# Output projections: a third of the weight tiles' low halves subtracted on GpSimd, and sums of squares added source by source

## The chip, the cores and the metric
The kernel runs on one core of a Trainium2 chip. The metric is the device time of one execution in microseconds (us), lower is better. Three timed runs of the kernel before gave 2628.65, 2626.24 and 2626.40 us, so the median is 2626.4 us. The execution that the profiler recorded took 2624.79 us, of which the span from the first to the last recorded instruction is 2623.0 us.

## The reference
The program computes two layers of a trunk over 256 latent tokens of width 2048, all in f32. Layer 0 is attention, layer 1 a long convolution ("hyena"); each ends in an output projection, and each is followed by a gated feed-forward block (ffn). What matters here:

```
xs = xs + g1 * (mix @ w_out)                       # output projection, 2048 x 2048; layer 0: attn_w_out, layer 1: hy_w_out
h  = rms(xs, norm2_g) * (1 + sc2) + sh2            # needs mean(xs^2) per token, over all 2048 columns
xs = xs + g2 * ((gelu(dwconv(h @ w_gate)) * (h @ w_val)) @ w_down)
```

g1, sc2, sh2 and g2 are vectors made by the "ada" products, s_lat @ ada_w + ada_b, one per layer and kind.

## The kernel before, in words
Every activation stands transposed, columns on the 128 partitions and 256 tokens along the free axis, as 16 pieces of 128x256. Each f32 product is made as three products of rounded halves: x = xh + xl and w = wh + wl, and wh*xh + wh*xl + wl*xh is summed in PSUM.

**One weight tile** is 256 rows by 512 columns of a weight matrix, stored as 128x1024 f32 (512 KB). `wload` (L326) issues its DMA from SyncE's queue into one of 6 `raw` buffers. `wsplit` (L331) makes the two halves: ScalarE rounds raw to `whi` (L334), VectorE subtracts, `wlo` = raw - whi (L335). There are three `whi` and three `wlo` buffers. `products` (L338) then issues 24 matmuls on TensorE for one tile, 8 with wh and xh, 8 with wh and xl, and 8 with wl and xh last, so `wlo` is wanted 16 matmuls after `whi`.

**The two output projections** are calls of `proj_out` (L1017), at L1163 with `w_out` and at L1321 with `hw_out`. Each has 32 weight tiles: a first pass over three groups of 512 rows, for one half of the columns and then the other (24 tiles), and a second pass over the last group (8 tiles). In the last group of a pass two tiles are taken together, and each column piece is finished by `evac` (L1023): VectorE multiplies the PSUM result by the gate and adds it to `xs` (L1026). In the second pass the piece is squared as well, on ScalarE; the first twelve squares are added up on VectorE into one tile, `sqacc` (L400), the last four stay single (L1030).

**What runs beside them.** `drive` (L315) calls generators between weight tiles. In both projections these are the ada products on VectorE (L486, a multiply with accumulation over 128x1024 f32, both inputs in SBUF), at 0.8 and 0.6 per step. Beside the first projection runs the end of attention (softmax and transposes) and, in its second pass, the filters of the convolution ("fill", L581 to L619: products on TensorE, multiplications and splits on VectorE and ScalarE). Beside the second runs the last of the convolutions ("conv", L1223).

**The sums of squares.** `rstd_of` (L376) sums over the partitions by matmuls: five sources (`sqacc` and four squares), each in two halves of 128 tokens, with the 128x128 piece as the weights and one column of ones as the moving operand. It goes through all sources for tokens 0 to 127, then again for tokens 128 to 255. VectorE reads the two columns (L384) and finds the reciprocal root in ten small steps (`newton`, L361); two matmuls (L391) spread it over the partitions, and `Normed.get` (L409) makes the input of the next stage. Nothing of the next stage's products can start before that.

**Order of the work.** The order on each engine is laid down when the program is built, by a list scheduler with priorities and a cost for each operation; `tc.high_priority()` and `tc.issue_after` (L485) steer it. At run time each engine works in that order and waits on semaphores. GpSimd has no work in the kernel after its first microsecond.

Of the kernel before, what the change touches and what calls it, by code (L numbers as in the profile page):

```python
# [16 lines left out]
ALU = mybir.AluOpType  # L17
AX = mybir.AxisListType

P = 128  # L20
# [175 lines left out]
def trunk_kernel(ctx, tc, out, xT, cT, cols, rows, f_w0, f_w12, f_w3, ada_w, ada_t, w_in, w_out, hw_in, hw_out,  # L196
                 wg, wv, wd, k_tab, k_fg, k_z, k_decay):
    nc = tc.nc
    V, A, PE, SP, G = nc.vector, nc.scalar, nc.tensor, nc.sync, nc.gpsimd
# [7 lines left out]
    def nm(s):  # L207
        uid[0] += 1
        return f"{s}{uid[0]}"
# [4 lines left out]
    def s2(shape, dt=F32, name="s"):  # L214
        return pool.tile(shape, dt, tag="s2", bufs=NS2, name=nm(name))
# [7 lines left out]
    def tiny(shape, name="t"):  # L223
        return pool.tile(shape, F32, tag="tiny", bufs=40, name=nm(name))
# [24 lines left out]
    def keep(shape, name, dt=F32):  # L249
        return pool.tile(shape, dt, tag=name, name=nm(name))  # L250
# [6 lines left out]
    ones = keep([P, P], "ones")  # L257
# [50 lines left out]
    def need(*what):  # L308
        for lj in what:
            ada_bg.drain(lj)  # L310
# [4 lines left out]
    def drive(gen, rate, ada_rate=0.0):  # L315
        up = isinstance(ada_rate, tuple)
        for now in gen:
            if now == "down":
                up = False
                continue  # L320
            ada_bg.step(0.0 if calm[0] else ada_rate if not isinstance(ada_rate, tuple) else ada_rate[0] if up else ada_rate[1])
            ev_bg.step(EV_RATE)
            fill_bg.step(fill_rate[0])
            bg.step(rate)

    def wload(src, tag="raw"):  # L326
        raw = pool.tile([P, 2, 512], F32, tag=tag, bufs={"raw": NRAW, "araw": NAR}.get(tag, NW), name=nm(f"raw_{lab[0]}_"))
        SP.dma_start(raw, src)
        return raw

    def wsplit(raw):  # L331
        hi = pool.tile([P, 2, 512], F32R, tag="whi", bufs=NW, name=nm(f"whi_{lab[0]}_"))
        lo = pool.tile([P, 2, 512], F32R, tag="wlo", bufs=NW, name=nm(f"wlo_{lab[0]}_"))
        A.copy(hi, raw)  # L334
        V.tensor_tensor(lo, raw, hi, op=ALU.subtract)  # L335
        return hi, lo

    def products(terms):  # L338
# [12 lines left out]
    def turn(bank):  # L351

        for i in range(4):
            with tc.issue_after(last(PE)):
                PE.transpose(bank[:, i * P:(i + 1) * P], ident, ident)
# [5 lines left out]
    def newton(y, v, n):  # L361

        t = small(n)
        V.tensor_scalar(t.bitcast(I32), v.bitcast(I32), 1, None, op0=ALU.logical_shift_right)
        V.tensor_scalar(y.bitcast(I32), t.bitcast(I32), -1, 0x5F1FFFF9, op0=ALU.mult, op1=ALU.add)

        V.tensor_tensor(t, y, y, op=ALU.mult)
        V.scalar_tensor_tensor(out=t, in0=t, scalar=-0.703952253, in1=v, op0=ALU.mult, op1=ALU.mult)
        V.scalar_tensor_tensor(out=y, in0=t, scalar=0.703952253 * 2.38924456, in1=y, op0=ALU.add, op1=ALU.mult)
        V.tensor_tensor(t, y, y, op=ALU.mult)  # L370
        V.tensor_tensor(t, t, v, op=ALU.mult)
        V.scalar_tensor_tensor(out=t, in0=t, scalar=-10.0 / 3.0, in1=t, op0=ALU.add, op1=ALU.mult)
        V.tensor_scalar(t, t, 0.375, 1.875, op0=ALU.mult, op1=ALU.add)
        V.tensor_tensor(y, y, t, op=ALU.mult)

    def rstd_of(accs, ps):  # L376

        pss = ps()
        n = len(accs)
        for tt in range(2):  # L380
            for i, a in enumerate(accs):
                PE.matmul(pss[:, tt: tt + 1], a[:, tt * P:(tt + 1) * P], ones[:, 0:1], start=i == 0, stop=i == n - 1)
        v = tiny([P, 2])
        V.tensor_scalar(v, pss[:, 0:2], 1.0 / D, EPS, op0=ALU.mult, op1=ALU.add)  # L384
        y = tiny([P, 2])
        newton(y, v, 2)
        pb = ps()
        dg = s2([P, T])
        for tt in range(2):
            V.tensor_scalar(dg[:, tt * P:(tt + 1) * P], ident, y[:, tt: tt + 1], None, op0=ALU.mult)  # L390
            PE.matmul(pb[:, tt * P:(tt + 1) * P], ones, dg[:, tt * P:(tt + 1) * P], start=True, stop=True)  # L391
        return pb[:, 0:T]

    def square_into(acc, x, first):
        if first:
            A.activation(acc, x, AF.Square)
        else:
            sq = s2([P, T])
            A.activation(sq, x, AF.Square)
            V.tensor_tensor(acc, acc, sq, op=ALU.add)  # L400
# [616 lines left out]
    def proj_out(w, passes, xsplit, gate, xs, accs, hook=lambda half, left: None):  # L1017


        acc = pool.tile([P, T], F32, tag="sqacc", bufs=2, name=nm("sqacc"))  # L1020
        accs.append(acc)

        def evac(final, half, banks, ct):  # L1023
            g = half * 8 + ct
            xt = xs[g // 4][:, g % 4]
            V.scalar_tensor_tensor(out=xt, in0=banks[ct // 2][:, (ct % 2) * T:(ct % 2 + 1) * T], scalar=gate[:, g:g + 1], in1=xt, op0=ALU.mult, op1=ALU.add)  # L1026
            if final and g < 12:
                square_into(acc, xt, g == 0)
            elif final:
                accs.append(s2([P, T], F32, "sq"))  # L1030
                A.activation(accs[-1], xt, AF.Square)

        def term(banks, ct, wh, wl, k2, xh, xl, k, first, last):
            c = ct % 4
            return (banks[ct // 2][:, (ct % 2) * T:(ct % 2 + 1) * T], wh[:, k2, c * P:(c + 1) * P], wl[:, k2, c * P:(c + 1) * P],
                    xh[:, k], xl[:, k], first, last)

        for p, (order, rings) in enumerate(passes):
            final = p == len(passes) - 1
            n = len(order)  # L1040
            for half in range(2):
                lab[0] = f"proj{p}{half}"
                banks = rings[half].four()
                if n > 3:
                    turn(banks[0])
                for i, kg in enumerate(order):
                    calm[0] = final and half == 1 and i == n - 1
                    if final:
                        hook(half, n - 1 - i)
                    xh, xl = xsplit(kg)  # L1050
                    src = lambda sub, j: w[kg * 2 + sub, half * 2 + j]
                    if i < n - 1:
                        for sub in range(2):
                            for j in range(2):
                                wh, wl = wsplit(wload(src(sub, j)))
                                products(term(banks, j * 4 + c, wh, wl, k2, xh, xl, sub * 2 + k2,
                                              i == 0 and sub * 2 + k2 == 0 and c % 2 == 0, False)
                                         for k2 in range(2) for c in range(4))
                                yield
                    else:  # L1060
                        for j in range(2):
                            ws = [wsplit(wload(src(sub, j))) for sub in range(2)]
                            for c in range(4):
                                ct = j * 4 + c
                                products([term(banks, ct, *ws[k // 2], k % 2, xh, xl, k, n == 1 and k == 0 and ct % 2 == 0, k == 3)
                                          for k in range(4)])
                                if c % 2:
                                    with tc.high_priority() if final else nullcontext():
                                        evac(final, half, banks, ct - 1)
                                        evac(final, half, banks, ct)  # L1070
                                    yield
# [50 lines left out]
    accs = []  # L1122
# [16 lines left out]
    def fill(dcs, at, rate):  # L1139

        def hook(*now):
            ftag[0] = HI4 if now[0] == 0 else LO4
            if dcs and now == at:
                fill_bg.add(filters(dcs), "fill")
                fill_bg.one()
                fill_rate[0] = rate
        return hook
# [12 lines left out]
        fill_rate[0] = 0.0  # L1160

    need((0, 2))
    drive(proj_out(w_out, OUT_PASSES, o_split, adaV[:, 0, 2], xs, accs, fill(DCS[1], (0, 0), FILL1)), O_RATE, O_ADA)  # L1163
    need((0, 2), (0, 3), (0, 4))
    g2 = gain_of(col("n2", 0, KT), adaV[:, 0, 4], "g2")
    main_done()
# [7 lines left out]
    accs = []  # L1174
# [143 lines left out]
        xs.append(t)  # L1318
    accs = []
    need((1, 2))  # L1320
    drive(proj_out(hw_out, OUT_PASSES, h2split, adaV[:, 1, 2], xs, accs), HO_RATE, HO_ADA)  # L1321
    need((1, 3), (1, 4))
    g2 = gain_of(col("n2", KT, KT), adaV[:, 1, 4], "g2b")
    with tc.high_priority():
# [24 lines left out]
```

## Time and profile before

| | |
|---|---|
| median of 3 runs | 2626.4 us |
| the profiled execution | 2624.79 us |
| its span | 2623.0 us |
| TensorE busy in the span | 2523.8 us (96%) |
| VectorE busy | 1965.9 us (75%) |
| ScalarE busy | 1258.7 us (48%) |
| GpSimd busy | 0.7 us |
| first output projection, about | 520 to 692 us |
| second output projection, about | 1758 to 1888 us |

In the rows the engines are PE (TensorE's matmuls), PEld (its weight loads), DVE (VectorE), ACT (ScalarE), POOL (GpSimd) and SP (SyncE). L335 is line 335 of the kernel. A group such as "wlo_proj<-raw_proj,whi_proj" says which tile is written and which are read; "idle before" is the time in which the engine stood still just before the instruction, with the engine and tile that ended it. Matmuls are pipelined: a matmul row starts when the one before it has gone in, so that the distance of two starts is the cost of one, and the duration in the row is longer.

### The profile page before, as it was taken

What the parts mean: (1) busy time and instruction counts of PE and PEld (TensorE: products, weight loads), DVE (VectorE), ACT (ScalarE), POOL (GpSimd) and SP (SyncE); (2) the same over time, 40 slices, a digit from 0 to 9 for tenths busy, and PEclk for the clock granted to TensorE, in tenths of its full rate; (3) what the DMA queues carried; (4) which work ended last, traced back from release to release, by engine and by line L of the source; (5) the groups of instructions that cost most, each with busy time, mean ns of one, the idle gap of its engine ahead of it and who ended that gap; (6) DMA issues with size and microseconds to landing.
All of it is one profiled execution on the core that took longest, in us unless ns stands there. A gap on an engine that the chain in (4) does not pass through costs nothing. (4 is left out here: it accounts for less than half of the span.)

```text
span 2623.0 us, 48116 instructions
## 1 busy us (share of the span) xinstructions
PE 2523.8 (96%) x19502; PEld 2349.2 (90%) x19502; DVE 1965.9 (75%) x3071; ACT 1258.7 (48%) x1801; POOL 0.7 (0%) x6
## 2 busy tenths in 40 slices
PE   6789999999799999999999999999899999999999
PEld 3458886678799999999999999998899999999999
DVE  6638859877888888888878778889876755556664
ACT  3352235664544444445545655554454444445543
POOL 0000000000000000000000000000000000000000
PEclk8799999999899999999999999999999999999999
DMA  9597876457599999998897565556778766666664
GB/s 312 197 348 250 273 252 230 146 175 253 167 331 326 332 324 328 326 333 310 291 337 262 183 196 177 177 169 224 235 255 272 251 194 194 194 194 193 194 209 138
DMA packets 176726, 639.19 MB, mean 244 GB/s; under 512 B 19735, under 2 KB 19832, under 8 KB 176504
## 3 DMA queue, kind: packets, MB, share of 16 engines
q1 hardware_dynamic: 174200, 627.74, 72.0%
q10 hardware_dynamic: 2304, 8.39, 0.8%
q8 instruction: 152, 2.49, 0.4%
q14 instruction: 70, 0.57, 0.1%
HBM read 623.47 MB, written 12.58 MB: 242 GB/s over the span
## 5 line engine op out<-in xcount | busy, mean ns | idle before, releaser
L334 ACT CAST whi_proj<-raw_proj 128x1024 fp32r<-128x1024 f32 x240 | 251.7, 1054 | 297.4 <-PE ps_proj L343 250.0
L335 DVE TENSOR_TENSOR wlo_proj<-raw_proj,whi_proj 128x1024 fp32r<-128x1024 f32 x240 | 292.0, 1221 | 135.8 <-ACT whi_proj L334 132.1
L486 DVE SCALAR_TENSOR_TENSOR araw_ada<-araw_ada,slB 128x1024 f32<-128x1024 f32 x320 | 387.5, 1217 | 0.0
L343 PE MATMUL ps_proj<-ph,whi_proj 128*128 128x256 f32 x1408 | 192.7, 277 | 1.1 <-ACT ph L358 1.0
L343 PE MATMUL ps_proj<-pl,whi_proj 128*128 128x256 f32 x1408 | 191.8, 277 | 0.0
L343 PE MATMUL ps_proj<-ph,wlo_proj 128*128 128x256 f32 x1408 | 191.3, 276 | 0.0
L343 PEld LDWEIGHTS ps_proj<-ph,whi_proj 128*128 128x128 f32 x1408 | 174.5, 188 | 2.8 <-ACT ph L358 1.7
L343 PEld LDWEIGHTS ps_proj<-pl,whi_proj 128*128 128x128 f32 x1408 | 174.3, 188 | 0.4 <-DVE pl L359 0.3
L343 PEld LDWEIGHTS ps_proj<-ph,wlo_proj 128*128 128x128 f32 x1408 | 174.3, 188 | 0.0
L334 ACT CAST whi_hy<-raw_hy 128x1024 fp32r<-128x1024 f32 x96 | 101.2, 1056 | 106.3 <-PE ps_hy L343 76.0
L335 DVE TENSOR_TENSOR wlo_hy<-raw_hy,whi_hy 128x1024 fp32r<-128x1024 f32 x96 | 116.3, 1221 | 45.9 <-ACT whi_hy L334 45.8
L343 PE MATMUL ps_hy<-hhi,whi_hy 128*128 128x256 f32 x768 | 109.6, 283 | 1.1 <-ACT hhi L423 1.1
L343 PE MATMUL ps_hy<-hlo,whi_hy 128*128 128x256 f32 x768 | 106.9, 280 | 0.0
L343 PE MATMUL ps_hy<-hhi,wlo_hy 128*128 128x256 f32 x768 | 105.3, 280 | 0.0
L343 PEld LDWEIGHTS ps_hy<-hhi,whi_hy 128*128 128x128 f32 x768 | 100.0, 191 | 3.4 <-ACT hhi L423 1.4
L343 PEld LDWEIGHTS ps_hy<-hlo,whi_hy 128*128 128x128 f32 x768 | 97.9, 190 | 0.8
L343 PEld LDWEIGHTS ps_hy<-hhi,wlo_hy 128*128 128x128 f32 x768 | 96.7, 190 | 0.1
L334 ACT CAST whi_kv<-raw_kv 128x1024 fp32r<-128x1024 f32 x40 | 41.9, 1050 | 112.7 <-PE ps_kv L343 93.3
L335 DVE TENSOR_TENSOR wlo_kv<-raw_kv,whi_kv 128x1024 fp32r<-128x1024 f32 x40 | 48.9, 1222 | 44.8 <-ACT whi_kv L334 44.5
L343 PE MATMUL ps_kv<-whi_kv,hhi 128*128 128x512 f32 x256 | 65.9, 399 | 0.0
L343 PE MATMUL ps_kv<-wlo_kv,hhi 128*128 128x512 f32 x256 | 64.0, 392 | 0.0
L343 PE MATMUL ps_kv<-whi_kv,hlo 128*128 128x512 f32 x256 | 63.8, 391 | 0.0
(9834 smaller groups left out, 7609.3 us busy)
## 6 DMA issues: line engine op xcount, KB each, us to landing
araw_ada<-ada_t SPq DMA_DIRECT2D x320, 512.0 KB, 5.2
raw_proj<-wd SPq DMA_DIRECT2D x176, 512.0 KB, 4.4
raw_hy<-hw_in SPq DMA_DIRECT2D x96, 512.0 KB, 3.7
raw_ada<-ada_w SPq DMA_DIRECT2D x46, 512.0 KB, 8.1
raw_kv<-w_in SPq DMA_DIRECT2D x40, 512.0 KB, 4.6
raw_q<-w_in SPq DMA_DIRECT2D x32, 512.0 KB, 4.1
raw_proj<-w_out SPq DMA_DIRECT2D x32, 512.0 KB, 4.7
raw_proj<-hw_out SPq DMA_DIRECT2D x32, 512.0 KB, 5.0
```

The costliest lines, as they stand in the source:

```text
L334: A.copy(hi, raw)
L335: V.tensor_tensor(lo, raw, hi, op=ALU.subtract)
L343: PE.matmul(o, ll if p == 2 else lh, rl if p == 1 else rh, start=first and p == 0, stop=last and p == 2, skip_group_check=True)
L486: V.scalar_tensor_tensor(out=raw, in0=raw, scalar=1.0, in1=slB[:, h * 1024:(h + 1) * 1024], op0=ALU.mult, op1=ALU.mult, accum_out=acc[:, h ...
```

## The change
Two edits. In `wsplit` a counter runs over all calls; while a flag is set, every call whose count is divisible by three gives its subtraction to GpSimd in place of VectorE. The flag is set around the two output projections only. In `rstd_of` the two loops are exchanged: for each source both token halves are added before the next source.

```diff
+    spare_lo = [0, 0]
+
     def wsplit(raw):
         hi = pool.tile([P, 2, 512], F32R, tag="whi", bufs=NW, name=nm(f"whi_{lab[0]}_"))
         lo = pool.tile([P, 2, 512], F32R, tag="wlo", bufs=NW, name=nm(f"wlo_{lab[0]}_"))
         A.copy(hi, raw)
-        V.tensor_tensor(lo, raw, hi, op=ALU.subtract)
+
+        spare_lo[1] += 1
+        (G if spare_lo[0] and spare_lo[1] % 3 == 0 else V).tensor_tensor(lo, raw, hi, op=ALU.subtract)
         return hi, lo
...
-        for tt in range(2):
-            for i, a in enumerate(accs):
-                PE.matmul(pss[:, tt: tt + 1], a[:, tt * P:(tt + 1) * P], ones[:, 0:1], start=i == 0, stop=i == n - 1)
+        for i, a in enumerate(accs):
+            for tt in range(2):
+                PE.matmul(pss[:, tt: tt + 1], a[:, tt * P:(tt + 1) * P], ones[:, 0:1], start=i == tt == 0, stop=i == n - 1,
+                          skip_group_check=True)
...
+    spare_lo[:] = 1, 0
     drive(proj_out(w_out, OUT_PASSES, o_split, adaV[:, 0, 2], xs, accs, fill(DCS[1], (0, 0), FILL1)), O_RATE, O_ADA)
+    spare_lo[0] = 0
...
+    spare_lo[:] = 1, 0
     drive(proj_out(hw_out, OUT_PASSES, h2split, adaV[:, 1, 2], xs, accs), HO_RATE, HO_ADA)
+    spare_lo[0] = 0
```

## Rows read from the trace of the kernel before

**Rows 1.** Part 1 of the page: busy us, share, instructions of each engine.

```profile
PE 2523.8 (96%) x19502; PEld 2349.2 (90%) x19502; DVE 1965.9 (75%) x3071; ACT 1258.7 (48%) x1801; POOL 0.7 (0%) x6
```

**Rows 2.** Windows view: the two projections, then 10 us of the second.

```profile
520.00:692.00 172.00, 157.25 (x1120) 137.13 (x1120) 135.66 (x273) 92.90 (x170) 0.00 (x0) 0.98 0.62 204
...
1758.00:1888.00 130.00, 119.05 (x923) 112.00 (x922) 117.18 (x205) 56.55 (x83) 0.00 (x0) 0.99 0.70 238
...
1830.00:1840.00 10.00, 8.14 (x70) 7.75 (x69) 10.00 (x19) 4.61 (x6) 0.00 (x0) 1.00 0.68 216
```

**Rows 3.** TensorE's waits, first projection: us in total, times, longest.

```profile
PE ps_proj L343 <- DVE wlo_proj L335: 4.3, 4, 2.4
...
PE ps_fill L347 <- DVE hf L590: 2.1, 2, 1.1
```

**Rows 4.** TensorE's waits, second projection, same columns.

```profile
PE ps_proj L343 <- DVE wlo_proj L335: 5.6, 7, 1.1
```

**Rows 5.** VectorE's groups in the first projection: busy us, mean ns, then idle before.

```profile
L335 DVE TENSOR_TENSOR wlo_proj<-raw_proj,whi_proj 128x1024 fp32r<-128x1024 f32 x32 | 38.9, 1218 | 9.6 <-ACT whi_proj L334 6.5 <-ACT oT L880 1.5 <-DMA w<-f_w 1.5
...
L486 DVE SCALAR_TENSOR_TENSOR araw_ada<-araw_ada,slB 128x1024 f32<-128x1024 f32 x23 | 28.0, 1216 | 0.0
```

**Rows 6.** VectorE's largest group in the second projection, same columns.

```profile
L335 DVE TENSOR_TENSOR wlo_proj<-raw_proj,whi_proj 128x1024 fp32r<-128x1024 f32 x32 | 38.3, 1216 | 2.0 <-ACT whi_proj L334 2.0
```

**Rows 7.** An undisturbed tile, from timelines: start us, us, engine, line.

```profile
612.46 1.06 ACT L334 CAST whi_proj<-raw_proj 128x1024 fp32r<-128x1024 f32 x1 [1.73 <-PE ps_proj L343]
...
613.55 1.23 DVE L335 TENSOR_TENSOR wlo_proj<-raw_proj,whi_proj 128x1024 fp32r<-128x1024 f32 x1 [0.52 <-ACT whi_proj L334]
...
620.38 1.07 PE L343 MATMUL ps_proj<-oh,wlo_proj 128*128 128x256 f32 x8
```

**Rows 8.** First projection, two tiles whose low half came late, same columns.

```profile
638.52 0.51 PE L343 MATMUL ps_proj<-oh,wlo_proj 128*128 128x256 f32 x2 [1.10 <-DVE wlo_proj L335]
...
660.68 1.05 ACT L334 CAST whi_proj<-raw_proj 128x1024 fp32r<-128x1024 f32 x1 [0.99 <-PE ps_proj L343]
...
672.22 1.21 DVE L335 TENSOR_TENSOR wlo_proj<-raw_proj,whi_proj 128x1024 fp32r<-128x1024 f32 x1
...
673.49 0.77 PE L343 MATMUL ps_proj<-oh,wlo_proj 128*128 128x256 f32 x2 [0.63 <-DVE wlo_proj L335]
```

**Rows 9.** Second projection, late low halves, same columns.

```profile
1802.34 2.00 ACT L334 CAST whi_proj<-raw_proj 128x1024 fp32r<-128x1024 f32 x2 [2.87 <-PE ps_proj L343]
...
1824.47 1.22 DVE L335 TENSOR_TENSOR wlo_proj<-raw_proj,whi_proj 128x1024 fp32r<-128x1024 f32 x1
...
1825.75 1.20 PE L343 MATMUL ps_proj<-h2h,wlo_proj 128*128 128x256 f32 x8 [1.13 <-DVE wlo_proj L335]
...
1833.43 1.19 PE L343 MATMUL ps_proj<-h2h,wlo_proj 128*128 128x256 f32 x8 [1.04 <-DVE wlo_proj L335]
...
1837.25 1.20 PE L343 MATMUL ps_proj<-h2h,wlo_proj 128*128 128x256 f32 x8 [0.82 <-DVE wlo_proj L335]
...
1869.65 0.51 PE L343 MATMUL ps_proj<-h2h,wlo_proj 128*128 128x256 f32 x2 [0.86 <-DVE wlo_proj L335]
```

**Rows 10.** GpSimd's two longest instructions, from its timeline.

```profile
0.73 0.20 POOL masks.py:197 MEMSET ident<- 128x128 f32 x1 [0.29 <-POOLq L1341]
...
1.01 0.29 POOL masks.py:199 TENSOR_SCALAR_AFFINE_SELECT ident<-ident 128x128 f32<-128x128 f32 x1
```

**Rows 11.** Sums of squares before the hyena stage, from timelines.

```profile
1437.56 0.72 ACT L1031 ACTIVATE sq<-xs 128x256 f32<-128x256 f32 x2
...
1439.62 0.28 PE L382 MATMUL ps_proj<-ones,sqacc 128*128 128x1 f32 x2
```

**Rows 12.** Sums of squares before the last ffn, from timelines.

```profile
1889.28 1.22 DVE L335 TENSOR_TENSOR wlo_ffn1.0_3356_20699<-raw_ffn1.0_3354_20696,whi_ffn1.0_3355_20698 128x1024 fp32r<-128x1024 f32 x1
...
1889.65 1.03 PE L382 MATMUL ps_proj<-ones,sq 128*128 128x1 f32 x8
...
1890.72 0.16 DVE L384 TENSOR_SCALAR t<-ps_proj 128x2 f32<-128x2 f32 x1 [0.22 <-PE ps_proj L382]
```

## The prediction, made before the changed kernel was run

> **What bounds the kernel now.** I read the totals first: TensorE is busy for 96% of the span, VectorE for 75%, and GpSimd for 0.7 us [rows 1]. So work off TensorE is worth only what TensorE waits for it. The windows view then gives the stages that the change touches: TensorE stands still for 172.0 - 157.25 = 14.8 us in the first projection and for 130.0 - 119.05 = 11.0 us in the second, while VectorE is busy for 79% and 90% of them, and in places without a gap [rows 2]. These 25.8 us, 1% of the kernel, are the most that any relief of VectorE can bring there. The waits view names what ends the idle time: a late `wlo` for 4.3 us in 4 waits and for 5.6 us in 7 [rows 3, 4]; other VectorE results come behind (`hf` of the fill, 2.1 us in its largest group [rows 3]).
>
> **What the first edit removes.** Before the first projection `wsplit` has been called 9 x 8 = 72 times (nine blocks of eight tiles for the inputs of attention), so its tiles 3, 6, ..., 30 go to GpSimd, 10 of 32. Between the projections come 176 + 88 calls for the ffn and 96 for hyena, 464 in all, so in the second it is tiles 1, 4, ..., 31, 11 of 32. That takes 21 x 1.22 us [rows 5, 6] = 25.6 us off VectorE. Most of it is worth nothing. In an undisturbed stretch ScalarE ends a `whi` at 612.46 + 1.06 = 613.52, VectorE its `wlo` at 614.78, and TensorE wants it at 620.38 [rows 7]: 5.6 us in hand.
>
> What counts are the waits of TensorE on a low half that moves. Counting the 32 subtractions of each stage in order of time, these are tile 24 (1.10 us) and tile 30 (0.63) of the first [rows 8], and tiles 13 (1.13), 16 (0.82) and 28 (0.86) of the second [rows 9]: 4.5 us together. Their `whi` is there early, and VectorE comes late because it works through other operations first: tile 30's `whi` ends at 661.73 and its subtraction begins at 672.22 [rows 8]; tile 13's `whi`, the second of a pair, ends at 1804.34 and its subtraction begins at 1824.47 [rows 9]. An engine with nothing else to do would begin at once. A sixth wait goes with them: tile 15 (1.04 us, at 1833.43 [rows 9]) is served by VectorE in a run without gaps that begins with tile 13's subtraction, and that run is now 1.22 us shorter. The other five waits, 9.9 - 4.5 - 1.0 = 4.4 us, I leave as they are: between the moved tile and those, VectorE waits for something else. First term: -5.5 us.
>
> **What a subtraction costs on GpSimd.** The trace has no such operation. Its nearest rows are a fill of 128x128 in 0.20 us and a selection with one input of 128x128 in 0.29 us [rows 10]. Eight times as many columns give 1.6 us from the fill, as the lower end; 2.3 us from the selection; and 4.6 us, if a second input doubles it, as the upper end. I take 2.3, as the selection is the nearest row; both ends go into the range. In the undisturbed stretch `wlo` would come at 613.52 + 2.3 = 615.8, or 618.1 at the upper end, both ahead of 620.38: covered by the two tiles ahead. On GpSimd's queue nothing stands but these operations, one for every three weight tiles; in the second projection 130 us / 32 tiles [rows 2, 6] make that one in 12 us, so none waits for another. The DMA into the raw buffer is released up to 3.4 us later, out of six buffers; this is hidden. The wait that is added, of TensorE on GpSimd, stands where that on VectorE stood.
>
> **What GpSimd may cost VectorE.** The trace shows no two-input GpSimd operation beside VectorE. At one end it costs nothing. At the other each one stops VectorE for all of its 2.3 us. That reaches TensorE only where VectorE runs without gaps, and seven of the 21 fall there (27 and 30; 13, 16, 19, 28, 31): 16 us. I take 0.4 us, near the lower end: the one case of two engines reading the same SBUF tiles that the rows show is ScalarE beside VectorE, and there VectorE's subtraction takes 1.22 us in the full stretch and 1.23 us in the quiet one [rows 7, 9].
>
> **The second edit** moves no work: 20 TensorE instructions before and after. It gains where the last square is late, since then four of them are left behind it and not up to twelve. Before the hyena stage all squares are done by 1438.28 and the first sum starts at 1439.62 [rows 11], after the fill's products: worth nothing, and the same pattern stands at 691 us. Before the last ffn the second half of the tokens ends at about 1890.7, and eight of its instructions take 1.03 us [rows 12]. Up to 1.0 us could go, but VectorE, which reads the sums at 1890.72, is busy with a subtraction for the next stage from 1889.28 to 1890.50 [rows 12]; if that stays ahead, only 0.2 us is left. I take 0.5, between them. At the start of the kernel the four sources are ready together: nothing.
>
> **Sum.** -5.5 + 0.4 - 0.5 = -5.6 us. On the profiled execution, 2624.8 us, that gives 2619.2; the median of the runs lies 1.6 us above that execution, so the forecast is 2626.4 - 5.6 = 2620.8 us. Its own range is 2617 (all of the 4.4 us of other waits, nothing else) to 2624.
>
> **Rivals.**
> *VectorE is stopped by GpSimd, and it evens out.* If a GpSimd subtraction holds up VectorE's operations with two inputs in SBUF, it meets them most of the time: subtractions and ada products alone are 66.9 of VectorE's 135.7 busy us in the first projection [rows 2, 5]. Each of the seven in the gapless places then takes some 2.0 of its 2.3 us from VectorE and gives back 1.22: +0.8 x 7 = 5.5 us, which cancels the first term: 2626 us. For it speaks that both engines would read `raw` and `whi` tiles from SBUF; against it, that the convolution's many operations on PSUM can pass. The Trainium skill states this rule (SBUF — State Buffer, section "Who interferes with whom"): a VectorE instruction with two SBUF inputs and a GpSimd one that reads SBUF use one shared port, and the second to come waits for the whole first; no run here shows it yet.
> *The wait only changes its name.* TensorE works in a fixed order, and behind a `wlo` stands often an `hf` or a `whi` that is as late; then 1 to 2 us are left, 2625 us. For it: the `hf` waits of the same stretch [rows 3]. Against it: the three waits at 1825 to 1837 have no other kind between them [rows 9].
> *Slower: GpSimd halts VectorE for longer than it relieves it.* Same place, the seven gapless subtractions. The change breaks even where one halts VectorE for 1.22 + 5.9/7 = 2.1 us, and loses beyond. At the upper end of the price, less the time that VectorE's PSUM operations fill, some 3.3 us: (3.3 - 2.1) x 7 = +8 us, 2634 us. For it: 10 us of ten in which VectorE has no gap [rows 2]. Against it: the 2.3 us of the nearest row.
> *More than forecast.* With VectorE free, the `hf` waits and part of the rest shrink too: -12 us, 2614 us.
>
> **How the numbers follow.** Forecast 0.43, evened out 0.22, new name 0.13, slower 0.15, more 0.07. A change of 0.2%, 5.3 us, is about what a measurement tells from none. Of the forecast's 0.43 I put 0.36 beyond that and 0.07 within, and all 0.07 of "more" with a little of the evened cases (0.02) also beyond: faster 0.45. Slower beyond it: 0.15 and 0.02 of the evened cases, 0.17. The rest, 0.38, is no change. The range 2613 to 2632 leaves out about 0.05 below and 0.12 above.
>
> **What would show it.** Right: GpSimd with 21 subtractions of about 2.3 us, TensorE's waits on `wlo` down from 9.9 to about 4.4 us in all, VectorE's subtractions still 1.22 us, and the sums before the last ffn ending nearer to the last square. Wrong: GpSimd operations of over 3 us, VectorE's two-input rows longer than 1.22 us or started late behind GpSimd, or the same idle time of TensorE under another releaser. Gaps at which the granted clock falls (its mean is 0.98 and 0.99 of 2.4 GHz in the two stages [rows 2]) would add to either side.

## The result, and the profile after

The changed kernel takes 2644.6 us (median of 6 runs, 2643.15 to 2649.79), the kernel before 2627.4 us beside it (6 runs): ratio 1.0067, 95% interval 1.0054 to 1.0080. It is 17 us slower; 2620.8 was forecast, and 2644.6 lies above the range of 2613 to 2632.

Part 1 of the page after answers to [rows 1].

```profile
PE 2539.6 (96%) x19502; PEld 2364.5 (89%) x19502; DVE 1970.3 (74%) x3051; ACT 1259.7 (48%) x1801; POOL 52.8 (2%) x26
```

VectorE has 20 instructions fewer (3071 to 3051), which is 24.4 us at 1.22 us each, and yet is busy for 4.4 us more. That is the first thing to see.

The windows view by stage, cut at the first matmul of each stage, before and then after (stretch, its length, busy us of each engine with instructions, granted clock, DMA share, GB/s). The rows are the first projection, the first ffn and the second projection.

```profile
538.70:700.61 161.91, 143.16 (x1054) 128.32 (x1053) 126.42 (x252) 79.85 (x143) 0.00 (x0) 0.96 0.60 194
700.61:1449.20 748.59, 742.03 (x6445) 737.18 (x6445) 631.02 (x882) 364.91 (x442) 0.00 (x0) 0.99 0.90 314
1765.90:1895.60 129.70, 114.17 (x875) 106.74 (x873) 116.83 (x210) 55.46 (x85) 0.00 (x0) 0.97 0.70 240
```
```profile
539.90:713.61 173.71, 147.23 (x1047) 133.46 (x1046) 130.38 (x243) 79.71 (x142) 24.45 (x9) 0.92 0.58 181
713.61:1468.80 755.19, 748.32 (x6444) 743.29 (x6444) 631.46 (x882) 364.96 (x442) 0.00 (x0) 0.99 0.89 311
1785.20:1919.72 134.52, 116.33 (x875) 107.92 (x873) 116.81 (x200) 56.01 (x85) 25.27 (x10) 0.96 0.68 231
```

The first projection is 11.8 us longer, the second 4.8. Of the 11.8, 7.7 are idle time of TensorE (173.71 - 147.23 against 161.91 - 143.16) and 4.1 are the same matmuls at a lower granted clock (mean 0.92 of 2.4 GHz against 0.96). The 6.6 us in the ffn are not the change's: matmuls follow each other more slowly in a part of that stage in this one execution, 5 us above the median, as they do in the profiled executions of three other kernels below (e_ffn, e_ffn6, e_one), and with the first edit alone the stage took 748.29 us.

GpSimd's group of subtractions (busy us, mean ns), and TensorE's waits in the two projections (us in total, times, longest), which answer to [rows 3, 4]:

```profile
L339 POOL TENSOR_TENSOR wlo_proj<-raw_proj,whi_proj 128x1024 fp32r<-128x1024 f32 x20 | 52.1, 2604 | 1845.9 <-ACT whi_proj L336 1845.9
```
```profile
PE ps_proj L347 <- DVE wlo_proj L339: 6.7, 3, 4.2
PE ps_proj L396 <- DVE s L395: 5.0, 1, 5.0
PE ps_attn L778 <- ACT pb L844: 4.6, 3, 1.9
PE ps_proj L347 <- POOL wlo_proj L339: 2.3, 1, 2.3
...
PE ps_proj L347 <- POOL wlo_proj L339: 3.6, 3, 1.3
PE ps_proj L347 <- DVE wlo_proj L339: 3.6, 2, 3.0
```

The waits on a low half rose from 9.9 to 16.2 us, and a new one is there, on the softmax (`pb`, 0.5 us before, 4.6 after). Its chain is in the timeline, ahead of two more places (start us, us, engine, line, and the idle time before it):

```profile
606.12 2.88 POOL L339 TENSOR_TENSOR wlo_proj<-raw_proj,whi_proj 128x1024 fp32r<-128x1024 f32 x1 [11.61 <-ACT whi_proj L336]
...
606.87 3.21 DVE L339 TENSOR_TENSOR wlo_proj<-raw_proj,whi_proj 128x1024 fp32r<-128x1024 f32 x1
...
610.00 0.68 DVE L838 TENSOR_REDUCE t<-ps_attn 128x1 f32<-128x512 f32 x1
...
611.74 0.20 DVE L841 TENSOR_SCALAR t<-t,sink 128x1 f32<-128x1 f32 x1
...
611.98 0.69 ACT L844 ACTIVATE pb<-ps_attn,t 128x512 f32<-128x512 f32 x1 [2.52 <-DVE t L841]
...
612.82 0.66 PE L778 MATMUL ps_attn<-ident,pb 128*128 128x128 f32 x4 [1.90 <-ACT pb L844]
...
1824.49 2.38 POOL L339 TENSOR_TENSOR wlo_proj<-raw_proj,whi_proj 128x1024 fp32r<-128x1024 f32 x1 [12.85 <-ACT whi_proj L336]
...
1824.75 0.48 DVE L1031 SCALAR_TENSOR_TENSOR xs<-ps_proj,adaV,xs 128x256 f32<-128x256 f32 x1
...
1825.14 2.00 DVE L1295 TENSOR_TENSOR z<-gt,z 128x256 f32<-128x256 f32 x1
...
1826.92 0.50 PE L347 MATMUL ps_proj<-h2h,wlo_proj 128*128 128x256 f32 x2 [1.26 <-POOL wlo_proj L339]
...
1853.06 2.46 POOL L339 TENSOR_TENSOR wlo_proj<-raw_proj,whi_proj 128x1024 fp32r<-128x1024 f32 x1 [13.32 <-ACT whi_proj L336]
...
1853.53 2.53 DVE L363 TENSOR_TENSOR h2l<-z,h2h 128x512 fp32r<-128x512 f32 x1
```

A VectorE subtraction that begins 0.75 us after GpSimd's takes 3.21 us and not 1.22. It ends at 610.08, 1.08 us after GpSimd's (609.00), so its work came after that. The row maximum (610.00) behind it is 2 us late, ScalarE waits for it, and TensorE for ScalarE. At 1825 a sum of 0.41 us takes 2.00, at 1853 a split of 0.68 takes 2.53. The update of `xs` at 1824.75, with one input in PSUM, runs beside GpSimd and keeps its 0.48 us. At 1826.92 TensorE waits for GpSimd itself. GpSimd stops too: at 606.12 VectorE's ada product (605.52 to 606.74) was still running, and GpSimd took 2.88 us, where alone it takes 2.35 to 2.41.

### The profile page after: what moved, and what is told of

Read it like the earlier page. It is cut to its first block, busy times and chain, and to the rows that moved or that the text cites. A ratio compares the mean times of both kernels' runs of the same rounds, so it can differ in the third digit from the quotient of the medians.

```text
span 2648.0 us, 48114 instructions
## 1 busy us (share of the span) xinstructions
PE 2539.6 (96%) x19502; PEld 2364.5 (89%) x19502; DVE 1970.3 (74%) x3051; ACT 1259.7 (48%) x1801; POOL 52.8 (2%) x26
## 5 line engine op out<-in xcount | busy, mean ns | idle before, releaser
L491 DVE SCALAR_TENSOR_TENSOR araw_ada<-araw_ada,slB 128x1024 f32<-128x1024 f32 x320 | 393.1, 1235 | 0.0
L339 DVE TENSOR_TENSOR wlo_proj<-raw_proj,whi_proj 128x1024 fp32r<-128x1024 f32 x220 | 272.4, 1241 | 144.8 <-ACT whi_proj L336 140.0
L339 POOL TENSOR_TENSOR wlo_proj<-raw_proj,whi_proj 128x1024 fp32r<-128x1024 f32 x20 | 52.1, 2604 | 1845.9 <-ACT whi_proj L336 1845.9
```

The source lines that it names most:

```text
L339: (G if spare_lo[0] and spare_lo[1] % 3 == 0 else V).tensor_tensor(lo, raw, hi, op=ALU.subtract)
L491: V.scalar_tensor_tensor(out=raw, in0=raw, scalar=1.0, in1=slB[:, h * 1024:(h + 1) * 1024], op0=ALU.mult, op1=ALU.mult, accum_out=acc[:, h ...
```

## The experiments

The theory after the result (lock): a VectorE operation with two inputs in SBUF waits until a GpSimd operation that reads SBUF is done, and that costs TensorE more than the relief gives. Its rivals: order (the instruction orders were laid down anew), path (GpSimd's 2.4 us stand where VectorE's 1.22 stood, and TensorE waits for that), and miscount (see "Which tiles move"). In the code below `third` stands for `spare_lo[0] and spare_lo[1] % 3 == 0`.

The stages of each kernel by the windows view, cut as above (first and second projection, us):

| kernel | length | VectorE busy | TensorE idle | granted clock |
|---|---|---|---|---|
| before | 161.9, 129.7 | 126.4, 116.8 | 18.8, 15.5 | 0.96, 0.97 |
| e_sums | 162.1, 129.1 | 126.4, 116.6 | 18.6, 14.7 | 0.96, 0.96 |
| e_gps | 173.0, 134.5 | 129.6, 116.7 | 26.2, 18.0 | 0.92, 0.96 |
| e_extra | 177.7, 149.8 | 142.5, 136.1 | 27.6, 26.7 | 0.93, 0.91 |
| e_left | 156.3, 123.1 | 116.7, 105.9 | 14.5, 8.7 | 0.95, 0.96 |
| e_fill | 160.2, 130.4 | 126.3, 116.6 | 17.0, 14.4 | 0.96, 0.96 |
| e_one | 166.1, 133.3 | 130.8, 122.1 | 20.0, 17.7 | 0.94, 0.96 |
| e_late | 162.7, 135.7 | 126.3, 116.9 | 17.1, 18.3 | 0.94, 0.94 |
| e_phase | 173.9, 142.6 | 129.3, 120.0 | 27.4, 24.1 | 0.92, 0.94 |
| e_hy | 162.0, 117.7 | 126.3, 98.6 | 18.7, 7.1 | 0.96, 0.98 |
| e_kv | 150.8, 119.0 | 104.9, 98.6 | 11.2, 7.2 | 0.96, 0.97 |
| e_kvsums | 150.8, 118.2 | 104.8, 98.5 | 11.2, 7.6 | 0.97, 0.98 |
| e_kvgps | 153.7, 123.2 | 102.0, 96.0 | 13.8, 11.6 | 0.97, 0.98 |

**The second edit alone.**

> The second edit alone (order of the sums of squares); every low half on VectorE. The orders of VectorE, ScalarE and the DMA queue are those of the kernel before, TensorE's differs at 8 of 19,073 positions. All theories: within 1 us of the kernel before (-0.5 us is what the prediction priced). If the second edit had a part in the loss, +2 us or more.

2626.1 against 2627.0 us, ratio 1.0004 (0.9986 to 1.0022): no part in the loss.

**The first edit alone.**

> The first edit alone (every third low half on GpSimd, 20 in all), sums in the old order. All three theories put the loss here: +16 to +18 us, as in the changed kernel. If the two edits only lose together, clearly less than +10.

Ratio 1.0069 (1.0048 to 1.0089), +18 us: the whole loss. In its trace 15 of VectorE's rows beside the 20 GpSimd operations are longer than usual, all with two inputs in SBUF, and what they are longer by adds up to 23.9 us. The relief is 24.4. VectorE gains nothing, as its busy time shows (1968.4 us in all, 1965.9 before).

**GpSimd's work without the relief.**

```
         V.tensor_tensor(lo, raw, hi, op=ALU.subtract)
+        if third:
+            scr = pool.tile([P, 2, 512], bfloat16, tag="scr", bufs=1)
+            G.tensor_tensor(scr, raw, hi, op=ALU.subtract)
```

> The kernel before with 20 GpSimd subtractions more, of the same two tiles at the same places, whose results (bfloat16, to a spare tile) nobody reads; VectorE still makes every low half, and TensorE, VectorE, ScalarE and the DMA queue issue in exactly the order of the kernel before. Lock theory (a VectorE operation with two SBUF inputs waits out a GpSimd one): VectorE loses some 1.5 to 2 us at each, half of that in stretches without slack: +8 to +20 us, with VectorE rows of over 2 us beside each GpSimd row. Order theory (the loss comes from the instruction orders that were laid down anew): 0 +- 1 us. Path theory (2.4 us stand on TensorE's path in place of 1.2): 0 +- 1 us.

Ratio 1.0132 (1.0111 to 1.0152), +35 us with the order of the other engines unchanged: the order theory can't explain that, nor can path. It is more than the 20 that I had given as the most. Nor is it that GpSimd, as one more reader, sets the `raw` and `whi` buffers free later: TensorE's waits on `whi` come to 3.9 us in the two projections of the kernel before, 4.6 here and 2.6 in the changed kernel. Three rows of its timeline:

```profile
1845.75 2.36 POOL L342 TENSOR_TENSOR scr<-raw_proj,whi_proj 128x1024 bf16<-128x1024 f32 x1 [15.90 <-ACT whi_proj L336]
...
1846.22 2.43 DVE L366 TENSOR_TENSOR yl<-m,yh 128x512 fp32r<-128x512 f32 x1 [1.03 <-ACT yh L365]
...
1848.71 0.50 PE L355 MATMUL ps_conv<-yl,dih 128*128 128x512 f32 x1 [1.85 <-DVE yl L366]
```

A split that TensorE is waiting for is stopped for 1.75 us (0.68 usually), and TensorE's wait is 1.85 us. VectorE's busy time rises by 16.1 and 19.3 us, the stages by 15.8 and 20.1: about one for one here. Of that, 8.8 and 11.2 us are idle time of TensorE; the rest are the same matmuls, busy for longer at a lower mean granted clock (0.93 and 0.91 against 0.96 and 0.97).

**The relief without GpSimd's work.** This run leaves out the low halves that the change moves.

```
+        if third:
+            return hi, hi
         V.tensor_tensor(lo, raw, hi, op=ALU.subtract)
```

> The low half of every third tile of the output projections is left out (the high half's tile is used in its place, same matmuls), so VectorE has 20 x 1.22 us less to do and GpSimd nothing; the orders are laid down anew as much as in the changed kernel (181 of VectorE's rows). Lock theory: -5 to -10 us against the kernel before, the relief that the prediction counted. Order theory: still slower than before, +5 to +12 us. Path theory: -5 us.

Ratio 0.9949 (0.9929 to 0.9969), -13 us, with orders moved as much as in the changed kernel (181 rows): the order theory falls as the cause of the loss. A small part of the loss is the new order's all the same. The longest wait on a low half in the changed kernel, 4.2 us at 692.55, stands in this run too, where GpSimd does nothing (first fence); in the kernel before it was 2.40 us (second):

```profile
673.05 0.80 PE L349 MATMUL ps_proj<-oh,wlo_proj 128*128 128x256 f32 x2 [4.14 <-DVE wlo_proj L341]
```
```profile
685.14 0.50 PE L343 MATMUL ps_proj<-oh,wlo_proj 128*128 128x256 f32 x2 [2.40 <-DVE wlo_proj L335]
```

The two halves add: +35 - 13 = +22 against +18 with both (12.6 to 23.4 by its interval). The relief itself is worth more than twice what I forecast.

**GpSimd writing only, and reading one tile.** In the place of the extra subtraction:

```
-            G.tensor_tensor(scr, raw, hi, op=ALU.subtract)
+            A.copy(scr[:, 0, 0:1], hi[:, 0, 0:1]); G.memset(scr, 1.0); G.memset(scr, 0.0)   # e_fill
+            G.tensor_copy(scr, hi)                                                          # e_one
```

> The kernel before with GpSimd writing only: at the same 20 places ScalarE puts one column of the high half into a spare bfloat16 tile, and GpSimd then fills that tile twice (128x1024, some 2 us for both by the small fill's row), reading no tile; TensorE, VectorE and the DMA queue issue in exactly the order of the kernel before. Lock theory in its narrow form (VectorE waits only for a GpSimd operation that reads SBUF): within 2 us of the kernel before, no VectorE row longer. Wide form (any GpSimd operation on SBUF stops VectorE's two-input ones): +20 to +36 us, as the extra subtractions (1.0132) made it.

> The kernel before with 20 GpSimd copies of the high half (one input of 128x1024, bfloat16 to a spare tile that nobody reads) at the places of the extra subtractions; the other engines issue in the order of the kernel before. If the lock lasts as long as GpSimd reads, whatever the number of inputs: VectorE rows stretched by about the copy's duration, and a loss of that over 2.4 us times 36 us (a copy of 1.2 us: +18 us). If only two-input GpSimd operations stop VectorE: within 2 us of the kernel before, no row longer.

e_fill: ratio 1.0009 (0.9993 to 1.0025), and none of VectorE's rows beside its 40 fills is longer. In the timeline an ada product, usually of 1.22 us, stands beside a fill of e_fill (first fence, with a subtraction) and beside a copy of e_one (second):

```profile
590.34 1.21 DVE L495 SCALAR_TENSOR_TENSOR araw_ada<-araw_ada,slB 128x1024 f32<-128x1024 f32 x1
...
591.30 0.95 POOL L343 MEMSET scr<- 128x1024 bf16 x1 [18.77 <-ACT scr L342]
...
591.82 1.20 DVE L339 TENSOR_TENSOR wlo_proj<-raw_proj,whi_proj 128x1024 fp32r<-128x1024 f32 x1
...
592.31 0.95 POOL L344 MEMSET scr<- 128x1024 bf16 x1
```
```profile
589.93 1.04 POOL L342 CAST scr<-whi_proj 128x1024 bf16<-128x1024 f32 x1 [17.56 <-ACT whi_proj L336]
...
590.17 1.88 DVE L493 SCALAR_TENSOR_TENSOR araw_ada<-araw_ada,slB 128x1024 f32<-128x1024 f32 x1
```

A fill of 0.95 us runs beside VectorE's two-input rows and lengthens none; a copy of 1.04 us, begun 0.24 us before the product, lengthens it by 0.67. So it is the reading, with one input as with two, and it lasts as long as the reading. The copies add 4.4 and 5.3 us to VectorE's busy time and 4.2 and 3.6 us to the stages; the ratio is 1.0017 (1.0000 to 1.0035), about 4.5 us, so that the time by itself is hardly told from none; the rows decide. I had expected 18 for a copy of about this length. A stop lasts only for what is left of the copy when VectorE comes to it, and that shrinks faster than the copy; 13 of the 20 copies came second and were stopped themselves (mean of all 1.51 us, 1.04 alone). That this is all of the difference is argued, not shown.

This is the rule of the Trainium skill (SBUF — State Buffer, section "Who interferes with whom"): a VectorE instruction with two SBUF inputs contends with a GpSimd instruction that reads SBUF, not with one that only writes it, and the second waits for the whole first. The trace agrees in each point, with 3.21 us in place of 1.22, 1.88 in place of 1.22 and 1.20 unchanged.

**The stops where TensorE has slack.** The extra subtractions, beside tiles of the first ffn:

```
-    if spare_lo[0] and spare_lo[1] % 3 == 0:
+    if spare_lo[0] and spare_lo[1] % 3 == 0 and 20 <= spare_lo[1] < 80:     # e_ffn, switched on in ffn(0) only
+    if spare_lo[0] and spare_lo[1] % 6 == 0 and 20 <= spare_lo[1] < 141:    # e_ffn6
```

> The 20 extra GpSimd subtractions (results read by nobody), put beside every third of the tiles 21 to 78 of the first ffn in place of the output projections; all other engines issue in the order of the kernel before. There VectorE is as busy (84%), but TensorE waits for nothing in over 650 us. Lock theory: VectorE is stretched as before, some 20 x 1 to 2 us, and the time stays within 2 us of the kernel before: the price is what TensorE waits for, not the stopped time. If stopped VectorE time costs by itself: +20 us or more.

> As the 20 extra subtractions in the first ffn, but beside every sixth tile (24 to 138), so that each has twice the stretch. At every third, VectorE was stretched by 41.5 us within 166 us that had 26.5 us free, and the time rose by about 8. If the price is what VectorE's free time can't take up: 41.5 us against some 51 free, within 2 us of the kernel before. If a stopped operation costs by itself: +8 us again.

e_ffn: ratio 1.0031 (1.0014 to 1.0047), +8 us where I had expected none. The windows view of the stretch in e_ffn, and of the same stretch of the kernel before:

```profile
755.00:921.00 166.00, 162.57 (x1402) 161.03 (x1401) 165.81 (x180) 70.73 (x86) 59.52 (x20) 1.00 0.88 300
```
```profile
745.00:911.00 166.00, 166.00 (x1467) 166.00 (x1467) 139.49 (x197) 78.64 (x94) 0.00 (x0) 1.00 0.93 326
```

VectorE had 26.5 us free in that stretch; its rows are longer by some 41 us (its busy time in the whole kernel by 38), and it is now full. TensorE waits there for VectorE's late low halves, 3.4 us in all, and the longest of these waits is (us in total, times, longest):

```profile
PE ps_ffn0.3_1526_7701 L350 <- DVE wlo_ffn0.3_1562_7949 L339: 1.3, 1, 1.3
```

The whole stage is 8.0 us longer in this execution (756.56 us against 748.59). The other 4.5 us are matmuls that follow each other more slowly at a granted clock of 1.00, which the changed kernel's profile has in this stage with no GpSimd work beside them; so 3.4 of the 8 us are seen as the price of the stops, and the rest is open. At every sixth tile VectorE's busy time rises by 32 us over a stretch with twice the room (TensorE is busy for 325.00 of 325.00 us there), and the ratio is 1.0006 (0.9993 to 1.0019). So stops cost nothing that can be measured where VectorE has the free time to take them up before TensorE wants its results, and something where it has not. The size does not follow from the free time alone: 41 - 26.5 would be 15 us. In the projections, where others wait for VectorE, they cost about the whole.

**A late low half without GpSimd.**

```
         V.tensor_tensor(lo, raw, hi, op=ALU.subtract)
+        if third:
+            A.copy(lo, lo)
```

> The kernel before with the low half of every third tile of the output projections made later, without GpSimd: VectorE makes it, and ScalarE copies it onto itself (some 1.06 us by its whi row, and a hand-over). Path theory (the 2.4 us of the GpSimd operation stand where VectorE's 1.22 stood, and TensorE waits for that): +5 to +12 us. Lock theory: 0 to +3 us.

Ratio 1.0011 (0.9995 to 1.0026), -1 to +7 us; its stages are 0.8 and 6.0 us longer. That doesn't decide between the two expectations. It bounds path, as far as this run's own new order hides nothing: under 7 of the 18 us, and it needn't be any. The waits on GpSimd's low halves (5.9 us in four waits after) bound it likewise, since 1.2 us of each is the longer operation: some 5 us.

**Which tiles move.** The front of this document and the prediction have an error: `spare_lo[:] = 1, 0` sets the count to zero ahead of each projection, so tiles 3, 6, ..., 30 move in the second as well, 20 operations in all and not 21. This run moves those that I had counted.

```
-    spare_lo[:] = 1, 0
+    spare_lo[:] = 1, 2     # at the second projection
```

> The changed kernel with the tiles that the prediction had counted: 3, 6, ..., 30 of the first projection and 1, 4, ..., 31 of the second (the changed kernel starts its count anew there, and moves 3, 6, ..., 30 again). Lock theory: the loss does not hang on which tiles move, +13 to +22 us. Miscount theory (the forecast failed because other tiles moved): about -5 us in the second projection, so 10 us faster than the changed kernel.

Ratio 1.0092 (1.0073 to 1.0111), +24 us: no faster than the changed kernel, and a little over the 22 that I gave as the most for the lock theory; in its profile the second projection takes 142.6 us against 134.5. The miscount did not make the forecast fail.

**A relief that leaves GpSimd out.** The kernel before makes no ada product in hyena, as `calm` stays set there, though TensorE waits for next to nothing in that stage (1.3 us in all).

```
-KV_ADA, Q_ADA, O_ADA, HY_ADA, HO_ADA = 1.9, 0.7, 0.8, 0.45, 0.6
+KV_ADA, Q_ADA, O_ADA, HY_ADA, HO_ADA = 1.9, 0.7, 0.8, 0.25, 0.0     # e_hy
+KV_ADA, Q_ADA, O_ADA, HY_ADA, HO_ADA = 2.6, 0.7, 0.0, 0.25, 0.0     # e_kv
+    calm[0] = False          # ahead of the loop over hyena, both
```

> No GpSimd: the kernel before with the 17 ada products of the second output projection moved ahead into the hyena stage (24 there, none in the projection), 17 x 1.30 = 22 us off VectorE in that stage. If VectorE's load there is worth what leaving out low halves showed (24.4 us for 12.6 us, half of it in this stage): -5 to -10 us; hyena itself, where TensorE waits for nothing and VectorE is busy for 83%, at most +2. If it is the low halves as such and not the load: 0 +- 2 us.

> As the last, and the 22 ada products of the first output projection are moved ahead into the projections for keys and values. Load theory: -10 to -18 us in all, and the first stage shortens by 5 to 8 us; rival: the stage of keys and values, which takes them over (VectorE 70 to 80% busy, 79% of the DMA time taken), gives back 3 us or more of it.

e_hy: 0.9965 (0.9947 to 0.9983), -9 us; the projection is 12.0 us shorter and hyena 3.1 longer (319.8 against 316.7), a little more than expected. e_kv: 0.9893 (0.9876 to 0.9910), 2600.9 us, -28 us and more than the 18 that I gave as the most. It leaves nothing out, and it beats both kernels. The windows view of e_kv, from the start through the first projection:

```profile
0.00:535.70 535.70, 487.42 (x2235) 347.08 (x2235) 400.68 (x809) 230.13 (x438) 0.70 (x6) 0.94 0.78 274
535.70:686.45 150.75, 139.51 (x1054) 127.09 (x1052) 104.92 (x209) 79.83 (x144) 0.00 (x0) 0.96 0.43 135
```

The first projection is 11.2 us shorter, and the part ahead of it, which took over 22 us of VectorE's work (400.68 busy against 378.58), gives nothing back: 535.70 us against 538.70.

**The two edits on that kernel.**

> The kernel with both ada moves (0.9893 of the one before) and the second edit. Both theories: the second edit is worth 0 to -1 us, so 0.988 to 0.990 of the kernel before.

> As the last, with every third low half of the output projections on GpSimd again: the change on a VectorE that has room (70% and 83% busy in the two stages). If the loss came only from VectorE being full there: 0 to -3 us against the last. Lock theory: the stopped operations still include those that TensorE waits for, and there is less to relieve: +5 to +15 us against the last.

With the second edit 0.9900 (0.9880 to 0.9919), no gain to be seen. With both 0.9944 (0.9922 to 0.9965): 10.7 us slower than the run beside it with the second edit alone (2612.7 and 2602.0 us), though VectorE was busy for only 70% of the first projection ahead of that (104.92 of 150.75 us in e_kv). GpSimd's subtractions lose even where VectorE has room on average, and even where they relieve it: its busy time in the whole kernel falls from 1966.4 to 1960.3 us. The two stages are 7.9 us longer than in e_kvsums, and TensorE's waits on GpSimd's own low halves (first and second projection) are 3.6 us of idle time that e_kvsums does not have (it has 3.6 us of waits on VectorE's low halves, and those go):

```profile
PE ps_proj L347 <- POOL wlo_proj L339: 1.2, 1, 1.2
...
PE ps_proj L347 <- POOL wlo_proj L339: 2.4, 2, 1.2
```

So on this kernel path may have a part beside lock; how the loss divides between them is not shown.

## Why the prediction was wrong

**The step that failed** is "What GpSimd may cost VectorE": 0.4 us, taken near the lower end of 0 to 16. The extra subtractions put it at 35 us, over twice the upper end: a VectorE operation with two inputs in SBUF waits until a GpSimd operation that reads SBUF is done. VectorE's two-input rows did get longer than 1.22 us, which the prediction had named as a sign of being wrong. Two of its reasons failed. The row that it leaned on, ScalarE beside VectorE at 1.23 us, says nothing of GpSimd. And "that reaches TensorE only where VectorE runs without gaps, and seven of the 21 fall there" counted full stretches of VectorE, but a stop costs just as much on an operation that TensorE, or ScalarE ahead of it, is waiting for: the softmax at 606 in the changed kernel, the split at 1846 in e_extra. The price also comes twice, as idle time and as longer matmuls at a lower mean granted clock (0.92 against 0.96 in the first projection).

**The relief, -5.5 us, was too small**: e_left gives -13. I counted only TensorE's waits on low halves [rows 8, 9], and in the second projection the three tiles that I counted as moved (13, 16, 28) stay with VectorE. Those that move and are waited for there are 12, 15 and 30 (0.57, 1.04 and 0.92 us); with the 1.73 us of the first projection that makes 4.3. In e_left TensorE's waits on low halves fall by 4.8 us, from 9.9 to 5.1; that this comes near the 5.5 is luck, since other tiles moved. But its idle time falls by 4.2 and 6.8 us: the other operations in VectorE's order come earlier as well, and the waits on them shrink too.

**GpSimd's duration, 2.3 us, held**: 2.35 to 2.41 us undisturbed, mean 2.60 with the stops. That the selection's row, taken eight times, came so near is luck in part: a one-input copy of this size took 1.04 us, and the fill 0.95 (to bfloat16) where its row had given 1.6. The later release of the raw buffers was hidden, as expected: TensorE's waits on `whi` did not grow.

**The second edit, -0.5 us**: not to be told from nothing. The timeline of e_sums, at the place of [rows 12]:

```profile
1886.59 0.81 ACT L1032 ACTIVATE sq<-xs 128x256 f32<-128x256 f32 x2
...
1887.06 1.51 PE L382 MATMUL ps_proj<-ones,sq 128*128 128x1 f32 x8 [0.65 <-ACT sq L1032]
...
1887.94 1.22 DVE L335 TENSOR_TENSOR wlo_ffn1.0_3356_20699<-raw_ffn1.0_3354_20696,whi_ffn1.0_3355_20698 128x1024 fp32r<-128x1024 f32 x1
...
1889.07 0.15 DVE L385 TENSOR_SCALAR t<-ps_proj 128x2 f32<-128x2 f32 x1
```

The last square ends at 1887.40 and the sums are read at 1889.07, 1.67 us later; before it was 1889.13 and 1890.72, 1.59 us. The sums themselves are done at 1888.57, but VectorE's subtraction for the next stage still stands ahead of the reading, the case that the smaller bound (0.2) had named.

**The rivals.** "VectorE is stopped, and it evens out" was right on VectorE (23.9 us stopped, 24.4 relieved) and wrong on the time: the relieved microsecond was worth about 0.6 (12.2 us of stage for 20.6 of VectorE's busy time in e_left), the stopped one about 1.0. "GpSimd halts VectorE for longer than it relieves it" had the right mechanism and sign at 0.15, but its break-even of 2.1 us per operation was wrong: the mean stop was 23.9/20 = 1.2 us and it lost 17. The name change was there only as a part: 5.9 us of waits went over to GpSimd.

## What to carry to other kernels

Before work goes to GpSimd, count VectorE's operations with two SBUF inputs in that stretch, and what waits for each: every one that comes to a GpSimd operation reading SBUF waits for its end, and twice the duration on GpSimd can take back all that VectorE is relieved of. Here the full engine was better relieved by moving its work in time, to a stage where less waits for it: the 39 ada products gave 28 us. An experiment with the added work whose result nobody reads, and one with the relieved work left out, price the two sides of such an exchange apart, and they added up here.

## What was not expected of the hardware

Alone, GpSimd took 2.35 to 2.41 us for a 128x1024 f32 subtraction, 1.04 for a one-input copy and 0.95 for a fill (both to bfloat16). The stop works both ways: a GpSimd subtraction lasts up to 3.41 us when it meets a VectorE operation already running. The profiled execution after has a stretch in the first ffn with mean matmuls of 281 ns in place of 276 at a granted clock shown as 1.00 in both, and so have those of e_ffn, e_ffn6 and e_one; what made that is open.
